# Moving turns between the stages of a one-core trunk layer: residual loads, a gated store, places for modulation rows

## The chip, the cores and the metric

The kernel runs on one core of one Trainium2 chip. A core has a matmul engine (PE, with its weight loads shown as PEld), a vector engine (DVE), a scalar engine (ACT), a general engine (POOL) and a queue engine (SP); 16 DMA engines move data between HBM and the on-chip memory. The metric is the device time of one launch in microseconds (us). Before the change it is 1829.59 us, the median of three runs (1829.15 to 1833.55).

## The reference, cut to what matters

The reference computes one layer of a diffusion trunk for 640 tokens: 512 noisy latent tokens and 128 context tokens, model width 1024, FFN width 2816.

```
m = silu(c) @ w_ada + b_ada                 # 9 modulation vectors of 1024 per token kind
x += m2/2 * swiglu(rms(x)*(1+m1)+m0)        # first half-step, weights w1a, w3a, w2a
h  = rms(x)*(1+m4)+m3
z  = mlstm(h) ;  a = diff_attention(h)      # memory branch || attention
y  = sigmoid(h@w_gm)*(z@w_brm) + sigmoid(h@w_gd)*(a@w_brd)
x += m5 * (y @ w_out)
x += m8/2 * swiglu(rms(x)*(1+m7)+m6)        # second half-step, weights w1b, w3b, w2b
```

`swiglu(h)` is `(silu(h @ w1) * (h @ w3)) @ w2`. The outputs are the layer's x, the new attention cache and the new memory states. All of it is float32 in and out.

## The kernel before, in words

**Arithmetic.** Every float32 factor is split into a high part H, rounded to the matmul's 32-bit format, and a low part L, the rest. A product is then three matmuls: H x H, L x H, H x L. A split costs one ACT copy (`act(..., AF.Copy)`, line 51 in the profile) and one DVE subtraction (`tt`, line 54). Weights arrive in float32 in a "raw" place of 128 x 2048, are split into a pair such as `wH`/`wL` or `ww`, and the raw place is then free for the next load. The tokens are handled in two halves of 320. In the FFN most products go through Winograd's form of 2 x 2 blocks: seven block products in place of eight, on sums of operand blocks. The block sums of an operand are named A11, A12, A21, A22, S1 to S4.

**Half-step.** `HalfStep.run_first` (first) and `HalfStep.run` (second) first do the "up" products: 20 work items, a w1 and a w3 granule for each block of 256 FFN columns. After each block the gated result SO = silu(.) * (.) is split and written to HBM by `store_g` (ACT copy into a place `g`, DVE subtraction, DMA stores on SP into `g_dram`). Places for `g` are called gA and gB. Then come the "down" products with w2, in groups of FFN blocks: group 0 as plain products in four steps j = 0..3 (each for 256 output columns), one middle group by seven products, and in the first half-step a last plain group. Their operands are read back from `g_dram` by `fetch(q, i)`, on POOL's queue (line 563) or on SP's. In each step j a weight two steps ahead is loaded (`load`), the next one is split (`split`), and the products add into the residual x (`add_residual`).

**Hooks.** `products` calls a hook `between(i, hf)` twice in each work item. In the first half-step the hook is `modulation`, with i shifted by 2; in the second it is `aside`. These put other work between the products: rows of modulation, loads of the residual, table loads.

**Modulation rows.** `Columns` computes 56 tiles of m: a tile is a row block of 512 KB of w_ada (`raw_a` or `ada<-in_w_ada_c`), multiplied and summed on DVE against silu(c) for the two token kinds (two instructions at line 753). `columns.place(n, csil, load, ahead)` says that the next n tiles go through a certain set of buffer places, and `ahead` how many loads may be out at a time; each `columns.tile()` computes one and starts the next load. A load's buffer is taken over in turn, so it waits for the products of the tile that had it before.

**Order.** A planner lays out each engine's instruction order from program order, simulated costs, and the availability of buffers. PE's order is as written. `tc.issue_after(ins)` puts what is issued inside it behind `ins` on the engine of `ins` only. A buffer of a new pool waits by default for all of the memory it covers; with `reuse_waits="tile"` it waits tile by tile. SP's queue and POOL's queue issue their DMAs in order, and all DMA engines serve both.

**After attention.** The four memory heads run as ten cells each, with rows of modulation at listed cells. Then `w_brd` products (d, evacuated by `d_evac`), 16 units, and `w_brm` products (m, evacuated by `m_evac`), in new PSUM banks (`ps4`) with a pool `gate`. Weights and, in this stretch, modulation rows both pass the two places of the pool `raw`. Then w_out, the second norm, and the second half-step.

Of the kernel before, what the change touches and what calls it, by code (L numbers as in the profile page):

```python
# [31 lines left out]
def tile_trunk(ctx: ExitStack, tc: tile.TileContext, a: dict):  # L32
# [421 lines left out]
    class HalfStep(Winograd):  # L454
# [37 lines left out]
        def store_g(self, SO, b):  # L492

            n = 4
            if b in self.summed:
                self.gated_sums(SO)
                n = 7
            for tag, c0, c1 in (("gA", 0, 4), ("gB", 4, 7)):
                if c0 < n:
                    g = self.fp.tile([128, 2048 if c0 else 2560], F32R, tag=tag, name="g")  # L500
                    g = g[:, : 2 * (c1 - c0) * HALF].rearrange("p (v s n) -> p v s n", v=2, s=c1 - c0)
                    act(g[:, 0], SO[:, c0:c1], AF.Copy)
                    tt(vec, g[:, 1], SO[:, c0:c1], g[:, 0].bitcast(F32), ALU.subtract)
                    for i in range(2):
                        nc.sync.dma_start(out=self.g_dram[c0:c1, :, i, b, :].rearrange("s p n -> p s n"), in_=g[:, i].bitcast(F32))
# [45 lines left out]
        def run_first(self, x, gate, final, between, ahead):  # L551
# [62 lines left out]
            def between_seven(i, hf):  # L614
                if (i, hf) == (2, 0):
                    at[2][1] = self.fp.tile([128, 2, 3, HALF], F32R, tag="gA", name="op")
                    fetch(2, 1)
                between(len(work) + 4 + i, hf)

            self.products(mid, between_seven, down[2][:2], prepared=True)  # L620
            for j in range(4):
                if j < 2:
                    down[2][j + 2].load()
                if j < 3:
                    down[2][j + 1].split(self.fp if j < 2 else None)
                for hf in range(1 if j else 2):
# [9 lines left out]
        def run(self, x, gate, final, ahead, aside):  # L636
# [133 lines left out]
    with ExitStack() as ph:  # L770
# [273 lines left out]
        def begin_columns():  # L1044
# [12 lines left out]
        places = []  # L1057

        def modulation(i, at):
# [29 lines left out]
        TILES = {(20, 1): 1, (21, 0): 1, (21, 1): 2, (22, 0): 1, (22, 1): 2, (23, 0): 1, (23, 1): 1, (24, 1): 1, (25, 1): 1, (26, 1): 1, (28, 1): 1}  # L1089

# [989 lines left out]
    in_order[0] = False  # L2080
    columns.place(18, csil2, load_columns_raw, 1)
    with written():
# [4 lines left out]
    for h in range(4):  # L2087
# [33 lines left out]
    def gate_of(src, g, mt, hf, **kw):  # L2121
        if (mt, hf) == (0, 0):
            sig[0] = load(shape=[128, 2, T], src=src[:, 2 * g : 2 * g + 2, :], name="sig", **kw)
            act(sig[0], sig[0], AF.Sigmoid)
        return sig[0][:, mt, half(hf)]
# [12 lines left out]
    for k in range(6):  # L2138
        if k % 3 == 0:
            raw = load(rawp, [128, 3, T], zT_dram[:, k : k + 3, :], tag="raw", name="z_raw")  # L2140
        act(zH[:, k], raw[:, k % 3], AF.Copy)
        tt(vec, zL[:, k], raw[:, k % 3], zH[:, k].bitcast(F32), ALU.subtract)
    while fill.q:
        fill.one()
        if columns.n:
            columns.tile()
    ml.close()
    mix.close()

    psum = Banks(ctx.enter_context(tc.tile_pool(name="ps4", bufs=1, space=PSUM)))  # L2150
    tmp = ctx.enter_context(tc.tile_pool(name="tmp", bufs=1))
# [287 lines left out]
```

## Time and profile before

| what | value |
| --- | --- |
| median of the runs | 1829.59 us (1829.15 to 1833.55) |
| profiled execution, its own time | 1827.84 us |
| its span | 1826.1 us |
| its mean granted clock of PE | 0.998 |
| PE busy | 1797.2 us, 98% |
| DVE busy | 1340.1 us, 73% |
| ACT busy | 879.9 us, 48% |
| first half-step, up products | to about 317 us |
| its down products | to about 469 us |
| attention, memory branch, branch products | to about 1283 us, and on with w_brm |
| second half-step, down products | from about 1677 us |

The profile shows one execution. PE is nearly always busy, so the time is PE's work, its few waits, and the clock that it is granted. The share of busy time of the other engines says little: what counts is which of them ends last before each of PE's waits. In rows of the timeline and of the chain, the first number is the start in us, the second the duration in us; `A<-B` is output from input by the program's names; what stands in brackets is the idle time before the instruction and what ended it.

### The profile page before, as it was taken

The page shows a single profiled execution, that of the slowest core. Times are in us where ns is not written, and L with a number is a line of the kernel's source. Part 1 is how long each engine was busy: PE and PEld are TensorE (multiplying, and loading weights), DVE is VectorE, ACT ScalarE, POOL GpSimd, SP SyncE. Part 2 cuts the span into 40 slices and gives each one's busy share as a digit, 9 for nine tenths or more (in the row PEclk, how much of TensorE's full clock was granted, in tenths as well). Part 3 has the DMA queues.
Part 4 walks back from the last instruction along what each step waited for, and adds up shares of the span by engine and source line. Part 5 has one row for each costly group of instructions (what it writes and reads, how often), then busy time and mean ns, then how long its engine had stood idle before and what let it go on. Part 6 is the DMA issues. An engine that isn't in the chain of part 4 may idle for free.

```text
span 1826.1 us, 30793 instructions
## 1 busy us (share of the span) xinstructions
PE 1797.2 (98%) x12622; PEld 1758.1 (96%) x12622; DVE 1340.1 (73%) x2188; ACT 879.9 (48%) x1510; POOL 34.2 (2%) x61
## 2 busy tenths in 40 slices
PE   8999999999999999999999999999999999999999
PEld 7999999999999999999999999999999999999998
DVE  6888896795986766475575649867767888896675
ACT  5654544223655454455465455672336545543232
POOL 0000000110000000000000000000000000000000
PEclk9999999999999999999999999999999999999999
DMA  8355567865234322112221055664642355659872
GB/s 325 109 196 187 173 228 290 314 248 204 83 138 141 122 67 87 63 62 86 82 89 71 21 176 168 215 247 170 256 158 80 133 174 187 208 179 339 312 271 79
DMA packets 131872, 307.71 MB, mean 169 GB/s; under 512 B 9809, under 2 KB 94033, under 8 KB 118801
## 3 DMA queue, kind: packets, MB, share of 16 engines
q1 hardware_dynamic: 121458, 262.20, 41.1%
q0 software_dynamic: 10128, 43.52, 6.4%
q8 instruction: 99, 1.62, 0.4%
q14 instruction: 43, 0.35, 0.1%
q10 hardware_dynamic: 144, 0.01, 0.0%
HBM read 238.14 MB, written 67.56 MB: 167 GB/s over the span
## 4 chain that ended last, share of the span: by engine, by line
PE 79%; DVE 9%; DMA 7%; ACT 3%; issue 2%; SPq 0%; DVEq 0%; ACTq 0%
PE ps_f L75 41%; PE ps_p L75 15%; PE ps_t L75 11%; PE sc L75 3%; PE ps_o L75 2%; PE ps_n L75 2%; DVE ww L54 2%; DMA raw_a<-in_w_ada_k 1%; PE ps_wT L78 1%; DMA raw<-in_w2b 1%; DMA raw_a<-in_w_ada_c 1%; DVE junk L753 1%; PE ps_u L75 1%; PE ps_qkT L78 1%; DVE raw_a L753 1%
## 5 line engine op out<-in xcount | busy, mean ns | idle before, releaser
L75 PE MATMUL ps_f<-S,ww 128*128 128x320 f32 x2124 | 342.1, 310 | 5.9 <-ACT u L51 2.1
L75 PEld LDWEIGHTS ps_f<-S,ww 128*128 128x128 f32 x2124 | 319.0, 188 | 9.9 <-DVE ww L54 5.4
L75 PE MATMUL ps_p<-hH,wH 128*128 128x320 f32 x672 | 213.3, 317 | 3.9 <-DVE y L54 3.1
L75 PE MATMUL ps_p<-hH,wL 128*128 128x320 f32 x672 | 208.4, 310 | 0.0
L75 PE MATMUL ps_p<-hL,wH 128*128 128x320 f32 x672 | 208.4, 310 | 0.0
L75 PE MATMUL ps_f<-hm,ww 128*128 128x320 f32 x1272 | 199.3, 310 | 2.9 <-DMA hm<-g_dram 1.9
L75 PEld LDWEIGHTS ps_f<-hm,ww 128*128 128x128 f32 x1272 | 190.0, 188 | 3.5 <-DMA hm<-g_dram 2.2
L75 PE MATMUL ps_t<-wH,hH 128*128 128x256 f32 x640 | 185.2, 289 | 0.9 <-DVE x L57 0.9
L54 DVE TENSOR_TENSOR ww<-raw,ww 128x2048 fp32r<-128x2048 f32 (+1 forms) x67 | 150.1, 2241 | 47.3 <-ACT ww L51 47.3
L75 PE MATMUL ps_t<-wH,hL 128*128 128x256 f32 x640 | 181.0, 283 | 0.9 <-DVE hL L54 0.9
L75 PE MATMUL ps_t<-wL,hH 128*128 128x256 f32 x640 | 180.8, 283 | 0.0
L51 ACT ACTIVATE ww<-raw 128x2048 fp32r<-128x2048 f32 (+1 forms) x67 | 125.5, 1873 | 105.2 <-PE ps_f L75 48.4
L75 PE MATMUL ps_f<-hm,wB 128*128 128x320 f32 x960 | 153.8, 309 | 0.0
L54 DVE TENSOR_TENSOR raw<-raw 128x1024 f32<-128x1024 f32 x168 | 145.1, 864 | 1.6
L75 PEld LDWEIGHTS ps_f<-hm,wB 128*128 128x128 f32 x960 | 144.1, 188 | 0.0
L75 PEld LDWEIGHTS ps_p<-hH,wH 128*128 128x128 f32 x672 | 127.0, 189 | 4.8 <-issue 3.3
L75 PEld LDWEIGHTS ps_p<-hL,wH 128*128 128x128 f32 x672 | 126.9, 189 | 0.3
L75 PEld LDWEIGHTS ps_p<-hH,wL 128*128 128x128 f32 x672 | 126.8, 189 | 0.0
L54 DVE TENSOR_TENSOR wL<-raw,wH 128x2048 fp32r<-128x2048 f32 x43 | 98.3, 2287 | 37.3 <-ACT wH L51 37.2
L75 PEld LDWEIGHTS ps_t<-wH,hH 128*128 128x128 f32 x640 | 122.3, 191 | 1.5 <-ACT nsq L51 1.1
L75 PEld LDWEIGHTS ps_t<-wH,hL 128*128 128x128 f32 x640 | 122.3, 191 | 1.1 <-DVE hL L54 1.1
L75 PEld LDWEIGHTS ps_t<-wL,hH 128*128 128x128 f32 x640 | 122.5, 191 | 0.4
(305 smaller groups left out, 3397.1 us busy)
## 6 DMA issues: line engine op xcount, KB each, us to landing
g_dram<-g SPq DMA_DIRECT2D x44, 640.0 KB, 6.6
raw_a<-in_w_ada_c POOLq DMA_DIRECT2D x25, 512.0 KB, 5.2
g_dram<-g SPq DMA_DIRECT2D x24, 480.0 KB, 8.2
raw<-in_w1b SPq DMA_DIRECT2D x11, 1024.0 KB, 4.8
raw<-in_w3b SPq DMA_DIRECT2D x11, 1024.0 KB, 6.2
raw<-in_w1a SPq DMA_DIRECT2D x10, 1024.0 KB, 4.8
raw<-in_w3a SPq DMA_DIRECT2D x10, 1024.0 KB, 6.3
raw_a<-in_w_ada_c SPq DMA_DIRECT2D x18, 512.0 KB, 3.8
```

Source lines behind the costliest of these rows:

```text
L51: return placed(nc.scalar.activation(*args, **kw))
L54: return placed(eng.tensor_tensor(out=out, in0=in0, in1=in1, op=op))
L75: tc.keep_in_program_order(nc.tensor.matmul(*args, **kw))
L78: tc.keep_in_program_order(nc.tensor.transpose(*args, **kw))
L753: placed(vec.tensor_tensor_reduce(out=junk, in0=raw, in1=self.csil[:, v, :], op0=ALU.mult, op1=ALU.add, scale=1.0, scalar=0.0, accum_out=m ...
```

## The change

The change moves work between stages. No product of the FFN, attention or memory is added or removed.

- **First half-step, residual.** `x` was read back from HBM in two loads of 1280 KB, one for each token half, at the hook i = 18. It is now read in four loads of 640 KB, one for each pair of column blocks: the first at i = 18, the others at the first hook of the down steps j = 0, 1, 2, on SP behind the weight load of that step.
- **Last gated store.** The ACT copy of `store_g` is remembered, and the weight split of each plain down step is put behind the last such copy on ACT. So is the table load `natural_log_exp` of the next hook.
- **Places for modulation rows, first half-step.** The first phase does 10 rows instead of 11, at a somewhat different list of work items. The second phase does 14 instead of 13, through four places (two in SO, two in gA) with four loads out, instead of two. The last operand of the third group, which takes gA too, is fetched one step later (before the fourth seven product instead of the third). The splits of the last group's weights are put behind the last vector instruction on DVE.
- **Memory branch.** 12 instead of 18 rows go through the raw places, all of them among the memory cells. Six then go through a place "so" of the memory pool, loaded on POOL, in the turns of the branch products. The new PSUM banks and the pool `gate` reuse memory tile by tile. `gate_of` asks for its place itself and loads on SP.
- **Second half-step, residual.** `x2` was read in four loads of 640 KB at the hook i = 18. The first stays there; the others are issued in the down steps j = 0, 1, 2 behind the weight load and ahead of the operand fetches of that step.

```diff
     # store_g
-    act(g[:, 0], SO[:, c0:c1], AF.Copy)
+    self.at_act = act(g[:, 0], SO[:, c0:c1], AF.Copy)
     # run_first, down steps
-    loaded = (down[0][j + 2] if j < 2 else mid[j - 2][0]).load()
+    loaded = self.loaded = (down[0][j + 2] if j < 2 else mid[j - 2][0]).load()
     if j < 3:
-        down[0][j + 1].split()
+        with tc.issue_after(self.at_act.ins):
+            down[0][j + 1].split()
     # between_seven
-    if (i, hf) == (2, 0):
+    if (i, hf) == (3, 0):
         at[2][1] = self.fp.tile([128, 2, 3, HALF], F32R, tag="gA", name="op")
         fetch(2, 1)
     # last group of the first half-step
-    down[2][j + 1].split(self.fp if j < 2 else None)
+    with tc.issue_after(self.at_vec.ins):
+        down[2][j + 1].split(self.fp if j < 2 else None)
     # run (second half-step), behind the weight load of step j
     with tc.issue_after(loaded):
+        aside(len(work) + j, 0)
         for i in ((A11, S1), (S2, A12), (S3,), ())[j]:
             fetch(1, i)
     # modulation rows
-    columns.place(11, csil, load_columns)
+    columns.place(10, csil, load_columns)
+    if at == 0 and 20 <= i < 23:
+        with tc.issue_after(hs.loaded):
+            reload_x(i - 19)
-    if at and (3 <= i < 18 and not (6 <= i < 14 and i % 2)):
+    if at and i in (3, 4, 5, 7, 9, 11, 14, 15, 16, 17):
         columns.tile(hs.at_vec)
-    for hf in range(2):
-        dma(box["x"][1][:, :, half(hf)], a["x"][:, :, half(hf)])
+    reload_x(0)
-    natural_log_exp()
+    with tc.issue_after(hs.at_act.ins):
+        natural_log_exp()
-    raws = [g[:, i * D : (i + 1) * D] for i in range(2)]
+    raws = [t[:, i * D : (i + 1) * D] for t in (g, fp.tile([128, 2 * 4 * HALF], F32, tag="gA", name="ada")) for i in range(2)]
+    raws.insert(0, raws.pop())
-    columns.place(13, places[0], load_columns)
+    columns.place(14, places[0], load_columns, 4)
-    TILES = {..., (22, 1): 2, (23, 0): 1, ...}
+    TILES = {..., (22, 1): 2, (23, 0): 2, ...}
     # memory branch
-    columns.place(18, csil2, load_columns_raw, 1)
+    columns.place(12, csil2, load_columns_raw, 1)
-    if n in ((3, 6, 8), (1, 3, 6, 8), (1, 4, 7), ())[h]:
+    if n in ((3, 5, 7, 8), (1, 3, 6, 8), (1, 3, 5, 7), ())[h]:
         columns.tile(m.at_vec)
+    def load_columns_so(src):
+        t = mp.tile([128, 2, T], F32, tag="so", name="raw_a").rearrange("p a t -> p (a t)")[:, :D]
+        nc.gpsimd.dma_start(out=t, in_=src)
+        return t, junk
+    columns.place(6, csil2, load_columns_so, 1)
-    psum = Banks(... name="ps4", bufs=1, space=PSUM)
+    psum = Banks(... name="ps4", bufs=1, space=PSUM, reuse_waits="tile")
-    with tc.tile_pool(name="gate", bufs=1) as gp:
+    with tc.tile_pool(name="gate", bufs=1, reuse_waits="tile") as gp:
     # second half-step, hooks
+    def reload_x2(g):
+        nc.sync.dma_start(out=x_pairs[g], in_=x2_dram[:, 2 * g : 2 * g + 2, :])
     elif (i, at) == (18, 1):
         x_pairs[:] = pairs("k", "x")
-        for g in range(4):
-            nc.sync.dma_start(out=x_pairs[g], in_=x2_dram[:, 2 * g : 2 * g + 2, :])
+        reload_x2(0)
+    elif at == 0 and 20 <= i < 23:
+        reload_x2(i - 19)
```

More of the change, by code (lines that the diff above doesn't have):

```diff
@@ L1053, in begin_columns, with reload_x @@
             ada_p.extend((pool, pool.tile([128, D], BF16, name="junk")))
-            columns.place(11, csil, load_columns)
+            columns.place(10, csil, load_columns)
         box = {}
         places = []
+        def reload_x(g):
+            dma(box["x"][1][:, 2 * g : 2 * g + 2, :], a["x"][:, 2 * g : 2 * g + 2, :])
         def modulation(i, at):
+            if at == 0 and 20 <= i < 23:
+                with tc.issue_after(hs.loaded):
+                    reload_x(i - 19)
             if i < 20:
@@ L1083, in load_columns @@
                         return raws[0], junk
-                    columns.place(13, places[0], load_columns)
+                    columns.place(14, places[0], load_columns, 4)
                 for _ in range(TILES.get((i, at), 0)):
                     columns.tile(hs.at_vec)
-        TILES = {(20, 1): 1, (21, 0): 1, (21, 1): 2, (22, 0): 1, (22, 1): 2, (23, 0): 1, (23, 1): 1, (24, 1): 1, (25, 1): 1, (26, 1): 1, (28, 1): 1}
+        TILES = {(20, 1): 1, (21, 0): 1, (21, 1): 2, (22, 0): 1, (22, 1): 2, (23, 0): 2, (23, 1): 1, (24, 1): 1, (25, 1): 1, (26, 1): 1, (28, 1): 1}
         def resid():
@@ L2122, in gate_of @@
         if (mt, hf) == (0, 0):
-            sig[0] = load(shape=[128, 2, T], src=src[:, 2 * g : 2 * g + 2, :], name="sig", **kw)
+            sig[0] = kw.pop("pool").tile([128, 2, T], F32, name="sig", **kw)
+            nc.sync.dma_start(out=sig[0], in_=src[:, 2 * g : 2 * g + 2, :])
             act(sig[0], sig[0], AF.Sigmoid)
@@ L2142, in tile_trunk @@
         tt(vec, zL[:, k], raw[:, k % 3], zH[:, k].bitcast(F32), ALU.subtract)
+    def load_columns_so(src):
+        t = mp.tile([128, 2, T], F32, tag="so", name="raw_a").rearrange("p a t -> p (a t)")[:, :D]
+        nc.gpsimd.dma_start(out=t, in_=src)
+        return t, junk
+    junk = mp.tile([128, 2, 258], F32, tag="N", name="junk", bufs=1).rearrange("p a n -> p (a n)")[:, : D // 2].bitcast(BF16)
+    columns.place(6, csil2, load_columns_so, 1)
     while fill.q:
@@ L2148, in tile_trunk @@
     mix.close()
-    psum = Banks(ctx.enter_context(tc.tile_pool(name="ps4", bufs=1, space=PSUM)))
+    psum = Banks(ctx.enter_context(tc.tile_pool(name="ps4", bufs=1, space=PSUM, reuse_waits="tile")))
     tmp = ctx.enter_context(tc.tile_pool(name="tmp", bufs=1))
```

## The prediction, on record before the result was known

> **What bounds the kernel now.** I read the busy shares first, then the matmul engine's waits by releaser, then the chain of work that ended last and the timeline around each wait.
>
> ```profile
> PE 1797.2 (98%) x12622; PEld 1758.1 (96%) x12622; DVE 1340.1 (73%) x2188; ACT 879.9 (48%) x1510; POOL 34.2 (2%) x61
> PE ps_p L75 <- DVE y L54: 3.1, 1, 3.1
> PE ps_f L75 <- ACT u L51: 3.0, 2, 2.1
> PE ps_f L75 <- DVE ww L54: 2.6, 4, 1.3
> PE ps_f L75 <- DMA hm<-g_dram: 1.9, 1, 1.9
> PE ps_f L75 <- DMA S<-g_dram: 1.3, 1, 1.3
> 1283.00:1287.00 4.00, 4.00 (x19) 4.00 (x18) 3.03 (x2) 0.09 (x1) 0.00 (x0) 0.57 1.00 376
> 1686.00:1690.00 4.00, 4.00 (x19) 4.00 (x19) 0.68 (x2) 0.00 (x0) 0.00 (x0) 0.59 1.00 404
> ```
>
> PE works 98% of the time. The change touches no matmul, so only the idle rest can be won. The wait rows give total us, number of waits and longest wait; the five that lie near the change sum to 11.9 us. The two window rows (span of the window, busy us and count of PE, PEld, DVE, ACT, POOL, then granted clock, DMA share, GB/s) add a second price: after the 3.1 us wait and after the 1.9 us wait PE is busy throughout but at a clock of 0.57 and 0.59, so 4 us do the work of 2.3: 1.7 us lost (4 x 0.43) and 1.6 us (4 x 0.41). All that can be had is therefore about 15 us, 0.8% of the time.
>
> **The end of the memory branch: rows through a place of their own.** The largest wait stands where the d products end and those with w_brm begin.
>
> ```profile
> 1247.47 1.13 DVE raw_a L753
> 1256.52 3.60 DMA raw_a<-in_w_ada_c
> 1271.58 1.17 DVE raw_a L753
> 1272.78 4.72 DMA raw<-in_w_brm
> 1277.60 1.92 ACT wH L51
> 1279.55 1.57 DVE wL L54
> 1281.76 0.50 DVE y L54
> ```
>
> Modulation rows and weights share two raw places here, in turn. The first w_brm weights are loaded only when the last row's product has freed a place (1271.58 + 1.17), land at 1277.5, are split by ACT and DVE until about 1281.8, and PE, whose new banks also wait for the last y (to 1282.3), starts then: the wait of 3.1. After the change 12 rows pass through the raw places earlier, among the cells of the memory stage, and the last 6 through the place "so", loaded by POOL. The raw places carry weights alone, so this load can start some 20 us earlier, its split is done before 1279, and banks and gate places that are released tile by tile no longer hold the first product for the last y. The row products are as many as before (18 and then 6). Gain 3.1 + 1.7 = 4.8; bounds 0 and 4.8; I take 4.8.
>
> ```profile
> raw_a<-in_w_ada_c POOLq DMA_DIRECT2D x25, 512.0 KB, 5.2
> ```
>
> The price: a row in "so" needs its load and two 1.13 us products before the next load starts. At the 3.6 us of 1256.52 that is 5.9 us, six of them 35 us, so a chain begun at 1247.5 ends near 1283, where the w_brm products already run; at the 5.2 us that POOL's row loads take on the mean of the whole kernel it ends near 1292. That is harmless unless something stands behind it on DVE (rival B). The 12 rows sit among cells whose weights wait in raw up to 20 us before use; I cost them at 0, cover being that slack.
>
> **The residual of the first half-step in pairs.**
>
> ```profile
> x<-in_x SPq DMA_DIRECT2D x2, 1280.0 KB, 10.7
> 294.00:304.00 10.00, 10.00 (x70) 10.00 (x69) 6.74 (x8) 5.60 (x8) 1.42 (x2) 1.00 1.01 348
> 306.70 11.49 DMA S<-g_dram
> 318.24 5.54 PE L75 MATMUL ps_f<-S,ww 128*128 128x320 f32 x36 [1.28 <-DMA S<-g_dram]
> ```
>
> Two loads of 1280 KB (2.62 MB) were issued near 293 into DMA engines that stay full (share 1.01, 348 GB/s). Now 640 KB (0.655 MB) go there. The 1.97 MB that go away are 1.97/348 = 5.7 us of transfer, and the operand at 306.70, the last of the backlog, lands that much earlier: its 1.28 us wait goes, and PE next needs a split that is done. Gain 1.3 (bounds 0, 1.3). The three later pairs go on SP behind the weight load of each j, and SP's operand fetch of the same j stands behind the pair: 0.65 MB/348 = 1.9 us later, for operands that come into use only after all four j, near 372. Cost 0.
>
> **The last gated store ahead of the split.**
>
> ```profile
> 317.86 1.92 ACT L51 ACTIVATE ww<-raw 128x2048 fp32r<-128x2048 f32 x1 [5.65 <-DMA raw<-in_w2a]
> 319.80 1.28 ACT L84 ACT_TABLE_LOAD   x1
> 319.81 2.29 DVE L54 TENSOR_TENSOR ww<-raw,ww 128x2048 fp32r<-128x2048 f32 x1 [4.08 <-ACT ww L51]
> 322.58 1.27 ACT L51 ACTIVATE g<-SO 128x1280 fp32r<-128x1280 f32 x1 [1.50 <-DVE ww L54]
> 330.66 0.60 PE L75 MATMUL ps_f<-S,ww 128*128 128x320 f32 x3
> ```
>
> This adds a wait: ACT must do the copy g<-SO before the split, and the copy needs its place freed by the store before. The split's readers are DVE and then PE at 330.66. Backwards from there, copy, table load, split and subtraction take 1.27 + 1.28 + 1.92 + 2.29 = 6.8 us, so the copy may start as late as 323.9; before it started at 322.58, and with less x traffic it comes earlier. Cost 0 (bounds 0 and 3, should the store land 3 us late); it frees SO earlier, and the new rows' loads start some 7 us earlier.
>
> **Four places for modulation rows, and the moved operand.**
>
> ```profile
> 319.00:372.00 53.00, 13.49 (x22) 1.00 0.90 323
> 372.00:397.00 25.00, 8.60 (x14) 1.00 0.81 296
> 397.00:412.00 15.00, 6.55 (x11) 1.00 0.37 123
> 185.88 2.29 DVE L54 TENSOR_TENSOR ww<-raw,ww 128x2048 fp32r<-128x2048 f32 x1 [2.25 <-ACT ww L51]
> 406.09 1.21 DVE L753 CUSTOM_DVE_ANT_0 ada<-ada,csil 128x1024 bf16<-128x1024 f32 x1
> 407.24 2.28 DVE L54 TENSOR_TENSOR ww<-raw,ww 128x2048 fp32r<-128x2048 f32 x1
> 409.96 8.45 DMA raw<-in_w2a
> 418.49 1.06 ACT L51 ACTIVATE wB<-raw 128x1024 fp32r<-128x1024 f32 x1 [4.05 <-DMA raw<-in_w2a]
> 419.97 0.42 ACT L51 ACTIVATE u<-ps_f 128x320 f32<-128x320 f32 x1
> 420.44 0.85 PE L75 MATMUL ps_f<-S,ww 128*128 128x320 f32 x4 [2.10 <-ACT u L51]
> ```
>
> The first three rows are windows of the row products alone (DVE's busy us, count, clock, DMA share, GB/s): DVE's share of them rises from 25% to 34% and 44%, a backlog, since with two places a row's load waits for the products of the row before. With four places, and one row fewer in the first phase at an early turn, three things follow.
> Near 408.5 PE waits about 1.0 of the 2.6 us of the ww row, because the subtraction at 407.24 stands behind row products; spread earlier they are gone: -1.0 (0 to 1.0).
> At 420.44 PE waits 2.10 for u, which ACT does behind wB, whose raw weights took 8.45 us from 409.96, beside rows and a 960 KB operand then in flight. With rows done earlier and the operand issued near 397 (gA is free only after the rows) instead, the weights come in time: -2.1. Bounds 0, if that operand falls into the same stretch, and 2.1. I take 2.1, since DMA share is only 0.37 from 397 to 412.
> At 185.88 the subtraction is late through sums that stood behind row products of 1.2 us; the tiles there are at other turns now: -1.3 (0, if the next turn collides instead, to 1.3).
> The last split, held behind a unit's addition, delays only DVE's subtraction: bounds 0 and 2.29 (one such). Together with the other turns of a newly planned order I take +1.0 for small new waits, range 0 to 4 (four of the size of those ww waits).
>
> **The residual of the second half-step in pairs.**
>
> ```profile
> x<-x_dram SPq DMA_DIRECT2D x4, 640.0 KB, 4.8
> 1660.00:1662.00 2.00, 2.00 (x16) 2.00 (x15) 2.00 (x2) 2.00 (x3) 0.00 (x0) 1.00 0.02 3
> 1662.00:1686.00 24.00, 22.09 (x151) 21.83 (x150) 14.83 (x20) 8.63 (x13) 0.00 (x0) 1.00 1.03 370
> 1669.88 2.75 SPq L97 DMA_DIRECT2D raw<-in_w2b  x2
> 1672.72 12.50 DMA hm<-g_dram
> ```
>
> Here the same edit speaks against itself. The four pairs were done before 1660, with the DMA idle after them (share 0.02). Now three of them go into the stretch that is full at 370 GB/s, the first right behind the weights of 1669.88 and so, most likely, ahead of the operand of 1672.72, for which PE already waits 1.9: 0.655 MB/370 = 1.8 us more, +1.8 (0 to 1.8). The other two pairs delay operands that come into use only after all four j: 0.
> The Trainium skill, "TensorE: Matmul & The Clock Gate" (Part 1), says the clock halves after about one idle window of 3.4 us. By it the 1.9 us wait costs no clock and one of 3.7 us does, 1.7 us more, a sum of -6.0. By it, too, the 3.1 us wait removed above would have cost no clock. The trace disagrees on both: its clock fell to 0.57 after 3.1 us and to 0.59 after 1.9 us, so here the price is paid before and after, and I do not add it.
>
> **Sum.** -4.8 -1.3 -1.0 -2.1 -1.3 +1.0 +1.8 = -7.7 us. The profiled execution took 1827.84, 1.75 below the median of 1829.59; from the median that gives 1821.9, and I say 1822.
>
> **Rivals.**
> A, the planner gives the rows' gains back: the three waits of the four places stay (+4.4), the rest comes: 1826.3, no change that can be measured. For it: each of these waits is a queue's order by a planner that lays all queues anew. Against: the first phase has one row fewer and four places shorten every chain.
> B, the other side: the planner puts the subtraction that makes the first wL behind the last row's products. With the chain of six rows ending at 1283, wL is ready 2.3 us later and PE starts at 1285.6 instead of 1282.4: a wait of 6.3 in place of 3.1, a clock that stays low twice as long (1.7 more), and none of the 4.8 won: 1821.9 + 4.8 + 3.2 + 1.7 = 1831.6. Each us by which the loads are slower than 3.6 adds six; from 4.3 us on it is above 1835.1, and at 5.2 it is 1841. It decides only if wL is ordered behind row five or six. For it: both use DVE in the same 40 us. Against: these weights can be split ten us before.
> C, the first x2 pair comes behind the operand: the wait at 1683 stays 1.9, 1820.1. For it the operand comes first in the program.
> D, the store lands late: the split waits to 3 us, 1825.
> E, the clock: if 1.9 us of waiting lost 1.6 us of clock, 3.7 us may lose as much again: 1821.9 + 1.6 = 1823.5. For it: the longer wait gives the throttle more idle time. Against: the 3.1 us wait lost no more than the 1.9 us one. The Trainium skill's rule named above gives nearly the same time (1823.6 by its 1.7).
>
> **How the numbers follow.** A measurement of this kernel can tell about 0.3% (5.5 us) from no change: faster is below 1824.1, slower above 1835.1. Forecast 1822: 0.44 (own range 1819 to 1824). C 0.10 and E 0.04 are faster too, 0.58 together. A 0.25, D 0.05 and 0.03 of B lie within the bound, 0.33. B's other 0.07, and 0.02 for waits that I haven't named, are slower, 0.09. Range 1817 to 1832: below, C with no new small waits and a little more; above, A with four us of small waits. It leaves out most of B and the ends of the others.
>
> **What would show it.** Right: the wait for y gone and the clock 1.0 from 1283 to 1287, the first w_brm load issued before 1260; the S wait gone; the u wait near 418 gone with its weights landing in under 6 us; the hm wait at 1683 grown to 3.7 with an x pair issued ahead of it. Wrong: a DVE wL behind a row product near 1283, a wait for ww between 319 and 331, or new waits of over 2 us between 330 and 470, where every queue is planned anew.

## The result and the profile after

The changed kernel takes 1840.22 us (1838.92 to 1843.84, 5 runs) where the kernel before takes 1829.59 us: a ratio of 1.0056 (95% interval 1.0037 to 1.0075), 0.56% slower. The forecast of 1822 us was wrong in sign, and the time lies above the range. The span of the profiled execution grew from 1826.1 to 1837.4 us, by 11.3 us.

The first line is the busy shares of the changed kernel; the next are PE's waits by releaser (total us, number, longest).

```profile
PE 1800.9 (98%) x12622; PEld 1762.6 (96%) x12622; DVE 1340.3 (73%) x2188; ACT 876.8 (48%) x1510; POOL 37.3 (2%) x67
...
PE ps_f L75 <- ACT u L51: 6.4, 1, 6.4
PE ps_p L75 <- DVE y L54: 5.9, 1, 5.9
PE ps_f L75 <- DMA hm<-g_dram: 3.9, 1, 3.9
...
PE ps_st L75 <- DVE P L54: 2.0, 1, 2.0
PE ps_f L75 <- DMA S<-g_dram: 1.2, 1, 1.2
```

Windows of the changed kernel (stretch, its length, busy us and count of PE, PEld, DVE, ACT, POOL, then granted clock, DMA share, GB/s):

```profile
384.00:395.00 11.00, 6.17 (x24) 6.17 (x25) 7.03 (x13) 2.23 (x4) 0.00 (x0) 0.53 0.41 143
...
1292.00:1299.50 7.50, 5.99 (x23) 5.99 (x24) 6.75 (x9) 0.00 (x0) 0.53 (x1) 0.54 0.52 169
...
1695.00:1702.00 7.00, 6.09 (x23) 6.09 (x24) 0.68 (x2) 0.00 (x0) 0.00 (x0) 0.51 1.02 406
```

The memory stage's own wait before the change, which the prediction did not show:

```profile
PE ps_st L75 <- DVE P L54: 0.5, 1, 0.5
```

Against the waits of before: the one for y grew from 3.1 to 5.9, the one for hm from 1.9 to 3.9, the one for P from 0.5 to 2.0; the waits for u were 3.0 in two places and are one of 6.4 in a third; those for ww fell from 2.6 to 0.5, now three of at most 0.2 us; S went from 1.3 to 1.2. Together +7.5 us. The three large waits each end in a stretch of about half clock. PE's 6.17, 5.99 and 6.09 us of work there lose about 47%, 46% and 49%: 2.9 + 2.8 + 3.0 = 8.7 us, where two stretches lost 3.3 us before, so +5.4. The sum, +12.9, is the 11.3 us of the span to within 1.6 us, of which 0.5 us are shorter waits in the opening, whose code is the same.

So there are three places to explain: near 382 (9.3 us with its clock, new), near 1288 (8.7 us, where 4.8 were), and near 1692 (6.9 us, where 3.5 were).

### The profile page after: what moved, and what is told of

Same layout as the page of the kernel before. It is cut to its first block, busy times and chain, and to the rows that moved or that the text cites. A ratio compares the mean times of both kernels' runs of the same rounds, so it can differ in the third digit from the quotient of the medians.

```text
span 1837.4 us, 30799 instructions
## 1 busy us (share of the span) xinstructions
PE 1800.9 (98%) x12622; PEld 1762.6 (96%) x12622; DVE 1340.3 (73%) x2188; ACT 876.8 (48%) x1510; POOL 37.3 (2%) x67
## 5 line engine op out<-in xcount | busy, mean ns | idle before, releaser
L75 PE MATMUL ps_f<-hm,ww 128*128 128x320 f32 x1272 | 203.5, 314 | 10.6 <-ACT u L51 6.4
L75 PEld LDWEIGHTS ps_f<-hm,ww 128*128 128x128 f32 x1272 | 193.8, 192 | 11.6 <-ACT u L51 6.6
L51 ACT ACTIVATE u<-ps_f 128x320 f32<-128x320 f32 x117 | 50.7, 434 | 160.4 <-PE ps_f L75 160.2
```

Source lines behind the costliest of these rows:

```text
L51: return placed(nc.scalar.activation(*args, **kw))
L75: tc.keep_in_program_order(nc.tensor.matmul(*args, **kw))
```

## The experiments

Each ratio is to the kernel before, run beside it on the same chip; the changed kernel itself is 1.0056. There were three chips, on which the kernel before had medians of 1830.39 us (beside e1, e2, e2b and e4), 1831.94 us (e3, e5, e7, e8) and 1831.27 us (f0, f1, f2, g1), so kernels of different groups are compared by their ratios.

| kernel | what differs | median us | ratio (95% interval) |
| --- | --- | --- | --- |
| e4_rows_stop | after, 4 rows in so, 8 in pairs | 1838.62 | 1.0048 (1.0030 to 1.0065) |
| e8_rows_in_cells | after, 14 rows in raw, 4 in so, 6 in pairs | 1833.52 | 1.0008 (0.9999 to 1.0017) |
| e5_memory_back | after, memory part undone | 1837.65 | 1.0037 (1.0023 to 1.0050) |
| g1_memory_alone | before, with e8's memory part alone | 1825.91 | 0.9973 (0.9964 to 0.9982) |
| e2_rows_later | after, two rows of turn 23 later | 1844.27 | 1.0076 (1.0057 to 1.0096) |
| e2b_weights_first | after, two operands behind the weights on SP | 1841.63 | 1.0061 (1.0039 to 1.0082) |
| e3_two_places | after, the part on places undone | 1841.82 | 1.0056 (1.0043 to 1.0069) |
| e7_x_back | after, first residual in two loads | 1838.08 | 1.0043 (1.0030 to 1.0056) |
| e1_x2_back | after, second residual all at i = 18 | 1837.95 | 1.0042 (1.0028 to 1.0057) |
| f0_cells_x2 | e8 and e1 together | 1827.39 | 0.9979 (0.9969 to 0.9988) |
| f1_behind_split | f0, rows held behind a subtraction | 1828.65 | 0.9988 (0.9979 to 0.9997) |
| f2_two_places | f0, 14 rows in two places | 1827.12 | 0.9982 (0.9973 to 0.9992) |

### Near 1288: rows ahead of an evacuation

The chain of work of the changed kernel there (start, us, what), then PE's first product with w_brm and DVE's timeline:

```profile
1284.42 6.11 DMA raw_a<-in_w_ada_c
...
1293.51 2.50 PE ps_p L75 x8
```

```profile
1283.90 0.31 PE L75 MATMUL ps_p<-hH,wH 128*128 128x320 f32 x1
...
1290.55 1.23 DVE L756 CUSTOM_DVE_ANT_0 junk<-raw_a,csil 128x1024 bf16<-128x1024 f32 x1 [5.82 <-DMA raw_a<-in_w_ada_c]
...
1291.82 1.23 DVE L756 CUSTOM_DVE_ANT_0 junk<-raw_a,csil 128x1024 bf16<-128x1024 f32 x1
...
1292.97 0.48 DVE L54 TENSOR_TENSOR y<-ps_p,sig 128x320 f32<-128x320 f32 x1
1293.37 2.28 DVE L54 TENSOR_TENSOR wL<-raw,wH 128x2048 fp32r<-128x2048 f32 x1
```

DVE stands idle for 5.82 us with an evacuation to do, because row five comes first in its written order and its load, which could only start when the one place was free, lands at 1290.5. Then come its two products, then y, then PE. PE was not waiting for the first w_brm weights: it had begun with them at 1283.90 and done one unit, to 1287.58, before it needed the bank that y empties. So the banks do come free tile by tile, as the change meant them to.

e4_rows_stop takes the last two rows out of so and gives them to the places that rows use in the next stage, the w_brm products (`load_columns_pair`):

```diff
-    columns.place(6, csil2, load_columns_so, 1)
+    columns.place(4, csil2, load_columns_so, 1)
-    columns.place(6, csil2, load_columns_pair, 1)
+    columns.place(8, csil2, load_columns_pair, 1)
```

> The changed kernel with four rows instead of six through the place so, and eight instead of six through the pair places of the w_brm products. Theory: the wait of 5.9 us near 1288 comes from the chain of rows through one place: the products of row five, whose load lands at 1290.5, stand on DVE ahead of the last d evacuation, whose bank PE needs. With no row after the fourth the evacuation is done near 1284, the wait and its clock loss (6.8 us at half rate, of which 5.7 while PE works) go: 8.8 us faster than the changed kernel, near 1831.4. Rival: PE waits there for the first weights with w_brm or for the new banks whatever the rows do; a wait of 2 us or more stays and at most 4 us are won.

The wait at 1288 is gone, but 1.5 us were won (1.0056 to 1.0048), not 8.8. The eight rows put the same fault at the end of the next stage: near 1346 PE waits for the high and low part of a result of the w_brm stage, the moving operand of the next products. PE's waits of this kernel, then its DVE timeline, where the subtraction that makes the low part stands behind the product of a row that had just landed:

```profile
PE ps_p L75 <- DVE hL L54: 2.0, 1, 2.0
...
PE ps_p L75 <- ACT hH L51: 1.5, 1, 1.5
```

```profile
1346.67 1.23 DVE L756 CUSTOM_DVE_ANT_0 junk<-raw_a,csil 128x1024 f32<-128x1024 f32 x1 [1.24 <-DMA raw_a<-in_w_ada_c]
...
1347.82 0.49 DVE L54 TENSOR_TENSOR hL<-ym,hH 128x320 fp32r<-128x320 f32 x1
```

e8_rows_in_cells moves those two rows the other way, into the last memory head:

```diff
-    columns.place(12, csil2, load_columns_raw, 1)
+    columns.place(14, csil2, load_columns_raw, 1)
-            if n in ((3, 5, 7, 8), (1, 3, 6, 8), (1, 3, 5, 7), ())[h]:
+            if n in ((3, 5, 7, 8), (1, 3, 6, 8), (1, 3, 5, 7), (1, 4))[h]:
-    columns.place(6, csil2, load_columns_so, 1)
+    columns.place(4, csil2, load_columns_so, 1)
```

> The changed kernel with two of the six rows of the place so moved back to the raw places, at cells 1 and 4 of the last memory head; four rows remain in so, six in the pair places. Theory: as with four rows before, no row product stands ahead of the last d evacuation, so the wait of 5.9 us near 1288 goes; and with six rows and not eight in the w_brm stage the waits of 1.5 and 2.0 us near 1345, which eight rows brought, do not come: 8.8 us faster than the changed kernel, near 1831.4. Rival: the two rows come back as waits among the memory cells or for the raw places (2 us or more between 1160 and 1290), and under 4 us are won.

The ratio falls from 1.0056 to 1.0008, 0.48% or 8.8 us, as expected, and the longest wait that PE has left between 1100 and 1430 us is 0.4 us.

e5_memory_back undoes the whole part (18 rows through raw, no so, banks and gate places without the release tile by tile):

> The changed kernel with the part on the memory branch undone: 18 rows through the raw places at the old cells, no place so, banks and gate places that wait for the whole memory. Theory: the wait of 5.9 us with 6.8 us of half clock near 1288 becomes the old one of 3.1 us with 3.4 us, so 4 us are won, near 1836. The wait of 2.0 us near 1072, which was 0.5 before the change, shows whether this part made it: 0.5 if so (another 1.5 us won), 2 or more if not. Rival: the wait at the first w_brm products is as long as in the changed kernel, for weights or banks, and nothing is won.

The old wait is back, at 3.8 us with one low stretch of 3.4 us, and the ratio is 1.0037: 3.5 us won against 4 expected. The wait for P stays at 1.8 us, so it is not this part's.

g1_memory_alone puts e8's form of the part, rows and tile-by-tile release together, into the kernel before and changes nothing else:

> The kernel before with the memory branch's part alone, with 14 rows in the raw places, 4 in so and 6 in pairs, and the tile-by-tile release of banks and gate places. Theory: what the prediction claimed for this part holds once no row stands ahead of the last evacuation: the wait of 3.1 us near 1280 and its 1.7 us of clock go, nothing else moves, 4.8 us (0.26%) faster than the kernel before, a ratio of 0.9974. Rival: the two more rows among the cells, or the rows in so, cost as much in new waits between 1070 and 1420, ratio 0.999 or more.

The two windows around the old wait, then PE's first product with w_brm and the last two y:

```profile
1279.00:1283.00 4.00, 4.00 (x30) 4.00 (x29) 1.71 (x4) 0.00 (x0) 0.53 (x1) 1.00 0.93 295
1283.00:1287.00 4.00, 4.00 (x30) 4.00 (x29) 3.31 (x6) 1.92 (x1) 0.00 (x0) 1.00 0.89 300
```

```profile
1283.72 0.31 PE L75 MATMUL ps_p<-hH,wH 128*128 128x320 f32 x1
...
1284.15 0.89 DVE L54 TENSOR_TENSOR y<-ps_p,sig 128x320 f32<-128x320 f32 x2
```

0.9973, the expected 0.9974: PE is busy through the whole of both windows, at clock 1.00. PE begins with w_brm 1.3 us before the last y is done (1285.04), so the release tile by tile has a share in the gain; no run has it alone. This kernel is faster than the one before and the changed one, and the fastest here by its median, though its interval overlaps those of f0 and f2. The single profiled executions differ by less than the medians, 1826.1 against 1824.3 us of span; the last section shows how far two executions of one kernel lie apart.

### Near 382: a weight load that lost its turn to two operands

The timelines of DVE, POOL, SP, ACT and PE of the changed kernel, in that order:

```profile
360.18 1.22 DVE L756 CUSTOM_DVE_ANT_0 ada<-ada,csil 128x1024 bf16<-128x1024 f32 x1
...
361.44 1.22 DVE L756 CUSTOM_DVE_ANT_0 ada<-ada,csil 128x1024 bf16<-128x1024 f32 x1
...
362.59 2.29 DVE L54 TENSOR_TENSOR ww<-raw,ww 128x2048 fp32r<-128x2048 f32 x1
...
361.64 0.71 POOL L563 DMA_DIRECT2D S<-g_dram  x1 [2.29 <-PE ps_f L75]
...
364.90 0.95 SPq L97 DMA_DIRECT2D raw<-in_w2a  x2
...
386.88 1.06 ACT L51 ACTIVATE wB<-raw 128x1024 fp32r<-128x1024 f32 x1 [10.54 <-DMA raw<-in_w2a]
387.84 0.61 ACT L51 ACTIVATE wC<-raw 128x512 fp32r<-128x512 f32 x1
388.36 0.42 ACT L51 ACTIVATE u<-ps_f 128x320 f32<-128x320 f32 x1
...
388.83 1.43 PE L75 MATMUL ps_f<-hm,ww 128*128 128x320 f32 x4 [6.37 <-ACT u L51]
```

The two products of a row, at 360.18 and 361.44, delay the subtraction at 362.59, which frees the raw place for the weights of 364.90. By then POOL's operand load is 3.3 us old. The weights come in two halves, and the later one lands at 386.8. ACT has the copies of them (wB, wC) ahead of u in its order, and PE needs u, so PE waits for weights whose own products come later. What holds them up is in the packets from 366 to 380 (queue: packets, MB, share):

```profile
q0 software_dynamic: 984, 4.58, 85.4%
q1 hardware_dynamic: 767, 0.77, 15.7%
```

POOL's queue (q0) and SP's (q1) take turns by packets, but q0's carry 4.65 KB each and q1's 1.0 KB, so the weights get 14% of the bytes. The Trainium skill, "DMA: Bandwidth & Descriptors" (Queues, rings and completion order), says that each DMA engine goes round its queues packet by packet; the trace agrees roughly, with 1.3 packets to 1.

e2_rows_later tries to clear the rows away:

```diff
-        TILES = {..., (23, 0): 2, (23, 1): 1, (24, 1): 1, (25, 1): 1, ...}
+        TILES = {..., (23, 0): 0, (23, 1): 1, (24, 1): 2, (25, 1): 2, ...}
```

> The changed kernel with two modulation rows moved from the hook of the last plain down step to the two hooks after the first seven products (23: 2 becomes 0, 24 and 25: 1 becomes 2). Theory: the new wait of 6.4 us near 382 comes from row products on DVE at 357 to 362, ahead of the weight subtraction that frees a raw place; the next weight load is then issued at 364.9, behind the two operand loads of 361.6 and 363.5, and takes 21 us. Without these two rows there the load is issued near 360, ahead of both operands, lands within 8 us, and the wait with its clock loss goes: 9 us faster than the changed kernel (near 1831), less up to 3 us if the moved rows bring back the waits near 408 and 418. Rival: the bytes alone decide (residual pairs, rows and operands share the DMA engines), the load takes about as long wherever it stands, and the wait stays over 4 us.

A miss: 1.0076. The rows of turn 23 weren't those ahead of the subtraction; it stayed behind the two products of another row (of turn 22), the load was issued at 366.78, 3.25 us after the first operand, and its halves landed after 14.3 and 19.5 us. The moved rows added waits for ww near 398 and 415 (1.8 us each). The condition of the test was not made, so it decides nothing between the theories. It shows something else, though. The later half landed at 386.7, no earlier than before, and yet PE's wait there fell from 6.4 to 2.7 us. ACT did one more u there, at 380.87, ahead of wB at 386.81. What late weights cost PE is thus also a matter of ACT's order. No run changed that order alone.

e2b_weights_first changes the order in the queues and leaves DVE's backlog ahead of the subtraction as it is:

```diff
-                    if (j, hf) == (3, 0):
-                        fetch(1, A12)
-                        fetch(1, S3)
-            fetch(1, A22)
+            def load_third(load=mid[2][0].load):
+                with tc.issue_after(load()):
+                    [fetch(1, i, nc.sync) for i in (A12, S3)]
+            mid[2][0].load = load_third; fetch(1, A22)
```

> The changed kernel with the row products left where they are, but the two operand loads of 361.6 and 363.5 taken from POOL's queue and put on SP's, right behind the weight load of 364.9. Theory: the crossing alone made the weights late. They land within 7 us, the wait of 6.4 us near 382 goes; the two operands now come some 6 us later, and as PE wants them at 375 and 377 a wait for them of 0 to 4 us may take its place. Time 1831 to 1836. Rival (the bytes decide, not the order): weights take over 12 us again and the wait at 382 stays over 4 us, with the operand waits on top, 1840 or more.

SP's timeline of this kernel, then its DMA issues (KB each, us to landing), then PE's waits:

```profile
365.35 1.02 SPq L97 DMA_DIRECT2D raw<-in_w2a  x2
366.47 1.23 SPq L563 DMA_DIRECT2D S<-g_dram  x2
```

```profile
raw<-in_w2a SPq DMA_DIRECT2D x2, 512.0 KB, 5.0
```

```profile
PE ps_f L75 <- DMA S<-g_dram: 5.3, 2, 4.1
```

Issued later than in the changed kernel, the weights take 5.0 us (median of the halves) instead of 18.2, and the wait for u is gone. The operand, now late, takes its place with 4.1 us, so the time is not better (1.0061, above the 1836 of the expectation). Ahead of the operands the weights are on time, and then an operand is late. This run changes the operands' queue together with the order; in e3 and f2, below, they stay on POOL's.

e3_two_places undoes the part on places (cut; the splits of the last group stay held as in the changed kernel):

```diff
-            columns.place(10, csil, load_columns)
+            columns.place(11, csil, load_columns)
-                if at and i in (3, 4, 5, 7, 9, 11, 14, 15, 16, 17):
+                if at and (3 <= i < 18 and not (6 <= i < 14 and i % 2)):
-                    raws = [... four places in SO and gA ...]
+                    raws = [g[:, i * D : (i + 1) * D] for i in range(2)]
-                    columns.place(14, places[0], load_columns, 4)
+                    columns.place(13, places[0], load_columns)
-                if (i, hf) == (3, 0):
+                if (i, hf) == (2, 0):
-        TILES = {..., (23, 0): 2, ...}
+        TILES = {..., (23, 0): 1, ...}
```

> The changed kernel with the part on places for modulation rows undone in the first half-step: 11 and 13 rows, two places with two loads out, the old turns, and the moved operand back at the third of the seven products. Theory: with two places fewer rows stand on DVE ahead of the subtraction that frees the raw place, the weight load of 364.9 is issued at or before the first operand load again, and the wait of 6.4 us near 382 with some 2.9 us of clock loss goes; the waits of 1.3, 1.0 and 2.1 us near 187, 408 and 418 come back: near 1835.5 us where the changed kernel has 1840.2. Rival: the residual pairs, which stay, make the weight loads late; the wait near 380 stays over 4 us and the time is 1840 or more.

The timelines of SP and POOL in this kernel, then its DMA issues:

```profile
362.63 0.93 SPq L97 DMA_DIRECT2D raw<-in_w2a  x2
...
364.00 0.70 POOL L563 DMA_DIRECT2D S<-g_dram  x1 [4.55 <-PE ps_f L75]
```

```profile
raw<-in_w2a SPq DMA_DIRECT2D x2, 512.0 KB, 4.0
```

With fewer rows ahead of it the load stands 1.4 us before the first operand and takes 4.0 us; there is no wait near 382. The part on places makes it, not the residual pairs, which stayed. The time did not fall, though (1.0056 again): the waits near 186, 408 and 418 came back with 1.3, 0.6 and 3.5 us, the last with 6.8 us of half clock, and new ones of 1.5 and 1.4 us stand near 1209 and 1759.

e7_x_back puts the first half-step's residual back into two loads, rows unchanged:

```diff
-            if at == 0 and 20 <= i < 23:
-                with tc.issue_after(hs.loaded):
-                    reload_x(i - 19)
 ...
-                    reload_x(0)
+                    for hf in range(2):
+                        dma(box["x"][1][:, :, half(hf)], a["x"][:, :, half(hf)])
```

> The changed kernel with the first half-step's residual in two loads of 1280 KB at the hook i = 18 again; the rows keep their four places. Theory (rows make the weights late): the wait near 382 stays between 4 and 7 us, and the wait for S near 314 grows from 1.2 to 3 to 5 us, since 1.97 MB more lie ahead of that operand: 1841 to 1844. Rival (the pairs' 640 KB in the stretch 307 to 351 make them late): the wait near 382 is under 2 us, and the time is 1836 or less.

The wait near 382 stays (4.4 us), as the theory says; but the wait for S did not grow. It is 1.3 us with 2.62 MB of residual ahead and 1.2 with less. The timelines of SP and POOL in e7, then its DMA issues:

```profile
289.97 1.37 SPq L97 DMA_DIRECT2D x<-in_x  x2
...
298.93 0.70 POOL L563 DMA_DIRECT2D hm<-g_dram  x1 [35.12 <-PE ps_f L75]
300.69 0.72 POOL L563 DMA_DIRECT2D S<-g_dram  x1 [1.06 <-PE ps_f L75]
304.22 0.70 POOL L563 DMA_DIRECT2D S<-g_dram  x1 [2.81 <-PE ps_f L75]
```

```profile
x<-in_x SPq DMA_DIRECT2D x2, 1280.0 KB, 11.1
```

The residual, issued by 290.7, has landed at 301.8, before the operand for which PE waits is issued at 304.22. What stands ahead of that operand are the two other loads of 1280 KB on POOL's own queue, and it lands 11.6 us after its issue; in the changed kernel the same three loads stand there, and it takes 11.5. The time expected, 1841 to 1844, was a miss: without the pairs in the down steps the ratio is 0.13% lower than the changed kernel's, which the intervals don't separate.

f1_behind_split, on top of f0 (below), moves two rows from turn 22 to later ones and holds those of turn 23 and after behind the subtraction (cut; `after_split` is a holder for an instruction):

```diff
-                    mid[0][0].sums()
+                    mid[0][0].sums(); self.at_vec = self.after_split(mid[0][0].split_at)
-        TILES = {..., (22, 0): 1, (22, 1): 2, (23, 0): 2, (23, 1): 1, (24, 1): 1, ...}
+        TILES = {..., (22, 0): 1, (22, 1): 0, (23, 0): 2, (23, 1): 2, (24, 1): 2, ...}
```

> The kernel with the two mended parts, and in the first half-step the two rows of turn 22,1 moved to 23,1 and 24,1, with all rows from turn 23 on held on DVE behind the subtraction that frees the raw place for the third middle weights. Theory: that subtraction then ends near 361 instead of 364.9, the weight load is issued ahead of both operand loads or between them, lands within 10 us instead of 21, and the wait of 5 to 6 us near 383 with some 2.9 us of clock loss goes: 1822 to 1826. Rival: rows that come later collect at the next weights (as the waits near 398 and 415 did when two rows were moved), and less than 4 us are won against the kernel with the two mended parts alone.

The timelines of POOL and SP in this kernel, then PE's waits:

```profile
362.82 0.71 POOL L564 DMA_DIRECT2D S<-g_dram  x1 [7.47 <-PE ps_f L75]
...
363.57 0.92 SPq L97 DMA_DIRECT2D raw<-in_w2a  x2
```

```profile
PE ps_f L75 <- ACT u L51: 7.9, 2, 7.1
```

A miss, and an instructive one: the load was issued 0.75 us behind the first operand, between the two as wished, and its halves still took 11.2 and 18.7 us; PE waits 7.1. The time is no better than f0's (0.9988 against 0.9979). Being between is hardly better than being behind.

f2_two_places gives the 14 rows two places, on top of f0:

```diff
-                    raws = [... four places in SO and gA ...]
-                    raws.insert(0, raws.pop())
+                    raws = [g[:, i * D : (i + 1) * D] for i in range(2)]
-                    columns.place(14, places[0], load_columns, 4)
+                    columns.place(14, places[0], load_columns)
```

> The kernel with the two mended parts, and in the first half-step two places with two loads out for the 14 rows instead of four; 10 rows in the first phase and the operand at the fourth of the seven products as in the changed kernel. Theory: two places alone keep the rows from running ahead, so the weight load stands before the operands (as with the whole part undone, where it landed in 4.5 us) and the wait near 383 goes; the rows' backlog comes back near 408 and 418, at most the 3.5 us of that run, since the operand of 960 KB no longer has its place early: 1823 to 1828. Rival: the waits at 408 to 420 are over 5 us with their clock loss, 1831 or more.

The load stands before the operands (362.74 and 364.11) and the wait near 382 is gone; near 418 there is one of 3.6 us, with 3.4 us of low clock. In all 0.9982 against f0's 0.9979: the same time, as far as the intervals tell, with the wait in another place.

### Near 1692: the residual pair

SP's timeline of the changed kernel:

```profile
1678.50 2.77 SPq L97 DMA_DIRECT2D raw<-in_w2b  x2
1681.32 1.58 SPq L2306 DMA_DIRECT2D x<-x_dram  x1
1683.00 1.53 SPq L652 DMA_DIRECT2D hm<-g_dram  x1
```

The pair stands between the weights and the operand for which PE waits. e1_x2_back undoes that:

```diff
         elif (i, at) == (18, 1):
             x_pairs[:] = pairs("k", "x")
-            reload_x2(0)
-        elif at == 0 and 20 <= i < 23:
-            reload_x2(i - 19)
+            for g in range(4):
+                reload_x2(g)
```

> The changed kernel with one part undone: all four pairs of the second half-step's residual are read at the hook i = 18 again, before the stretch whose DMA engines are full. Theory: the first pair, issued between the weights and the operand for which PE waits, costs the growth of that wait from 1.91 to 3.87 us and a second clock window of 3.4 us at half rate, so this kernel is about 3.5 us faster than the changed one (near 1836.7 us where that one has 1840.2), its wait for the operand near 1690 is 1.9 us again, and the clock is low there for 3.4 us and not 6.8. Rival: the operand is late for another reason (the later start of the whole stage, other queue order), the wait stays near 3.9 us, and the time stays within 1 us of the changed kernel.

From PE's waits of this kernel:

```profile
PE ps_f L75 <- DMA hm<-g_dram: 2.4, 1, 2.4
```

The wait is 2.4 us (1.9 expected) with one low stretch of 3.4 us instead of 3.9 with 6.8. The ratio is 1.0042: 2.6 us less than the changed kernel's, against 3.5 expected; the intervals alone would not settle it, the wait does. In all eight kernels with the pair there it is 3.5 to 4.0 us, in the six without it 1.9 to 2.5.

f0_cells_x2 is e8's and e1's edits together:

> The changed kernel with two of its parts mended: the rows of the branch stage as 14 in the raw places, 4 in so and 6 in pairs, and the four pairs of the second half-step's residual all at i = 18 again. Theory: the two waits are independent, so their savings add: 6.7 us for the first and 2.3 us for the second from 1840.2, near 1831, and only the wait near 382 and the one near 1072 are left of the loss. Rival: one of the two gains is given back elsewhere, 1833.5 or more.

0.9979: 14.1 us won from the changed kernel, where 9 were expected and the two ratios added make 11.4; the intervals don't separate these. The kernel is faster than the one before although the wait near 382 is still 5.2 us. Part of the surplus may lie in the clock: in the profiled execution, the fastest of its twelve, the wait for hm is 2.3 us and costs none (windows of f0, then g1, then the kernel before):

```profile
1685.00:1689.00 4.00, 4.00 (x29) 4.00 (x28) 1.21 (x4) 0.63 (x1) 0.00 (x0) 1.00 1.00 403
```

```profile
1683.00:1686.00 3.00, 0.46 (x3) 0.35 (x3) 0.83 (x1) 0.00 (x0) 0.00 (x0) 1.00 1.03 416
1686.00:1690.00 4.00, 4.00 (x29) 4.00 (x28) 0.76 (x3) 0.19 (x1) 0.00 (x0) 1.00 1.00 404
```

```profile
1685.90:1689.30 3.40, 3.40 (x15) 3.40 (x14) 0.68 (x2) 0.00 (x0) 0.00 (x0) 0.50 1.02 416
```

## Why the prediction was wrong, point by point

- **Memory branch (-4.8, measured about +3.9).** The step that failed is "harmless unless something stands behind it on DVE", by which the chain of rows cost nothing: the last y stood behind row five. The sum for the chain was also too short. Its loads took 4.0 to 7.8 us, not 3.6, and row five ended at 1293.0, 9.1 us after PE's first product with w_brm, where all six rows had been reckoned to end 3.7 us after it (1283 against 1279.3). Rival B, given 0.10, had the mechanism and the place, with one error in the name: what PE needed was the bank of the last y, not a wL. That its wait of 6.3 us comes so near the measured 5.9 is partly luck: the rows were later than it reckoned, and PE could do one unit with w_brm, 3.7 us, before it had to wait. The gain claimed for the rest of the part was right: without the late rows it is 4.9 us (g1, 0.27%) of the 4.8 forecast. The early w_brm load came as said, issued at 1250.8 and split by 1278.8.
- **Four places (-4.4 together, measured about +5 with its clock).** The waits near 187, 408 and 418 went, as forecast. What the step left out is that rows which can be loaded earlier are also multiplied earlier, in front of whatever DVE has next. The two products of one row made a subtraction late, that made a weight load change places with an operand load, and the new wait near 382 cost 6.4 us and 2.9 us of clock. e3 and f2 show that the number of places makes it; e2b, e3 and f2 show that the weights are on time when their load stands ahead of the operands. The prediction's own list of failures had "new waits of over 2 us between 330 and 470", but no price. Rival A had the old waits stay; they went, and a new one took their gain. In size it was right: by the runs the places are worth nothing (f0 against f2), and neither is the whole part but for the held splits (the changed kernel against e3, both 1.0056), since without it the old waits come back, the one near 418 longer than before.
- **First residual in pairs (-1.3, measured -0.1).** The step that failed is "the operand at 306.70, the last of the backlog, lands that much earlier". The residual was not ahead of that operand: issued by 293.2, it took 10.7 us and had landed at 303.9, before 306.70. The backlog was POOL's own, two loads of 1280 KB, which the change did not touch; e7 shows the same wait with the whole residual back.
- **Gated store (0) and its wait.** Right: no wait for ww stands between 319 and 331, and the copy began at 312.88, far from the latest start that the prediction allowed, 323.9. No run undid this part alone.
- **Second residual in pairs (+1.8).** Right in mechanism and near in size: the wait grew by 2.0 us, with the pair where it was expected, and by 1.5 us against e1. Its clock was wrongly left out: the low stretch doubled, 3.0 us lost for 1.6, so rival E's price (1.6, measured 1.4) came on top of the forecast.
- **Small waits (+1.0).** The wait for P near 1072 grew by 1.5 us, and one of 0.9 near 1784 went. The first stayed between 0.8 and 3.8 us in all kernels derived from the changed one, with the memory part or without it, and was 1.0 in g1. Which change of the loads' order or of the data's place causes it stays open.

The sizes of single waits were mostly right; what failed was the order in which in-order engines and queues would do the work.

## What to carry to other kernels

A buffer that lets side work start earlier also lets it stand in front of main work on the same in-order engine: for each place added, list what comes next on that engine and who waits for it. Two queues that share the DMA engines by packets are not one line: here a load in packets of 1 KB had to be issued before a load in packets of 4.65 KB, or it waited for nearly all of it. Before a load is called the backlog of another, its landing should be set against the other's issue. And a change of several parts should be costed with its parts apart: here one part, mended by moving two rows, was worth 0.27%, and the others together cost 0.37% (e5).

## What was not expected of the hardware

- The same two loads of 512 KB take 3.4 and 4.5 us when issued 1.4 us ahead of the operand loads on the other queue (e3), 11.2 and 18.7 us when issued 0.75 us behind the first of them (f1), and 15.0 and 21.5 us when issued 3.3 us behind (the changed kernel).
- Whether a wait costs clock is not a matter of its length alone. 1.9 us before the change cost a stretch at 0.50; 2.3 us in f0 and 2.5 us in g1, at the same place in the program, cost none. In the clock records of the traces the low stretches are 3.4, 6.8 or 10.2 us long, and the full ones between them are whole multiples of 3.413 us (in f0 1430.18 us, 419 of them). The Trainium skill, "TensorE: Matmul & The Clock Gate" (Part 1), has a window of 3.4 us that runs free of the kernel. The lengths agree. When the borders are counted on from a low stretch, the 1.9 us before the change lie inside one window (1682.5 to 1685.9), and the two waits that cost nothing are cut by a border: f0's at 1682.7 into 0.8 and 1.5 us, g1's at 1684.0 into 0.9 and 1.6 us. No run moved a wait against a border on purpose, and it is no sharp rule: the wait of 2.0 us near 1072 in the changed kernel lies almost wholly in one window and cost nothing.
- So a price of 1.7 us for a wait of about 2 us is one that a few us of shift elsewhere can add or remove, and the next execution too. The 18 executions of the unchanged kernel beside e1 had granted clocks from 0.994 to 1.0 and took from 1825.67 to 1838.65 us; a profile shows one of them.
